# Hybrid decoder step: six weight buffers for the down products, half-size tiles for the sums, and loads of the next chunk's operands kept behind weight loads

## The chip, the core and the metric

The kernel runs on one core of one Trainium2 chip. The metric is the device time of one execution in microseconds (us). The kernel before took 3053.38 us, the median of three runs (3050.13 to 3064.35).

## The reference, cut to what matters

One layer of a hybrid decoder is computed for 512 prompt tokens and 8 sample tokens that share all weights (520 columns). The change lies in the last part, the feed-forward net:

```
FFN_HIDDEN = 5632
h2 = rms_norm(x, n2)
x = x + (jax.nn.silu(h2 @ wg) * (h2 @ wu)) @ wd
...
return (rms_norm(x, norm_f), ...)
```

`wg` and `wu` are 2048 x 5632 and `wd` is 5632 x 2048, all float32. The change touches only `... @ wd`, the down products.

## The kernel before, in words

**Precision.** Every product is made of three matmuls of split numbers: a weight block is split into a high part (`whi`, written by ACT at L1358) and the rest (`wlo`, written by DVE in `lo_part`, L70), the moving operand likewise, and hi*hi, hi*lo and lo*hi are added in PSUM (L1363).

**Seven products in place of eight.** The feed-forward products run through `strassen` (L1332), which multiplies a 2 x 2 arrangement of weight blocks `a11, a12, a21, a22` with seven operands named B11, B21, T2, T1, T3, T4 and B22. One call is called a step here. A step of the down products takes two weight tiles (`raws`, one for each of two output columns of blocks; the first holds a11 and a12, the second a21 and a22), and `kp` rows of block pairs. In order it makes:

- part A: a12 x B21 into PSUM tile `pz`, then a11 x B11 into `px`;
- part B: the sum s1 = a21 + a22 (POOL, L1342), s2 = s1 - a11 (DVE, L1352, into PSUM, named `sm`), then s2 x T2 into `px`, s1 x T1 into `py`; s4 = a12 - s2 (DVE, L1352, named `se`), s3 = a11 - a21 (POOL), s3 x T3 into `px`;
- part C: a22 x T4 into `px`, s4 x B22 into `py`.

After most products DVE adds PSUM to an accumulator in SBUF (`ac`, L1622). `run` (L1393) interleaves neighbours: part A of a step, part C of the step before, part B of the step. So on PE the order is A(j), C(j-1), B(j), A(j+1), C(j), ... The last reader of a step's second weight tile is the split of a22 in part C.

**The down products** (`streams`, L1682) go through the hidden dimension in six chunks of `CHUNKS = (3, 4, 4, 4, 3, 4)` block pairs (called chunks 1 to 6 here), and in each chunk through 8 steps, one for each pair of output blocks. A step of kp = 4 has 7 x 4 x 3 = 84 matmuls, one of kp = 3 has 63. The seven operands of a chunk come from DRAM (`load_x`, L1580, into halves of `wx` or into `hs` tiles, 1040 KB each at kp = 4); those of the next chunk are loaded while this chunk runs, one load behind each step in program order. The weights of a step (`load_w`, L1592) are two loads of 512 KB (kp = 4) or 384 KB (kp = 3) into `raw_c`, cut into four buffers taken in turn (L1598): two steps' worth. The tiles of the sums (`s`) come from pool `sp`, three buffers of 8 blocks, allocated for the up and gate products (kp = 8) and used on by the down products, which need half of it.

**What sets the order.** A scheduler places the instructions of each engine ahead of time, in an order fixed for the run; each engine then works through its list and waits at an instruction until its inputs are there and its buffer is free. All loads and stores are issued by one queue, SP's, in its own fixed order. `tc.keep_in_program_order` forbids the scheduler to move an instruction ahead of those that stand before it in the program on the same queue. When the first `hs` tile is needed (`hs`, L1545), the pools of the up and gate products are closed and their memory is given to `hs`.

Of the kernel before, what the change touches and what calls it, by code (L numbers as in the profile page):

```python
# [9 lines left out]
F32 = mybir.dt.float32  # L10
# [7 lines left out]
P = 128  # L18
# [4 lines left out]
HF = T // 2  # L23
# [10 lines left out]
def hybrid_step_kernel(  # L34
# [9 lines left out]
    nc = tc.nc  # L44
# [1094 lines left out]
    t = g_s5  # L1139
# [95 lines left out]
    XS = {}  # L1235
# [3 lines left out]
    def parts(x, q):  # L1239
        return x[:, q, 0:HF], x[:, q, HF:T]  # L1240
# [88 lines left out]

    todo = []  # L1330

    def strassen(A_, kp, X, parts_of, sp, rep):  # L1332

        groups = [(q0, min(4, kp - q0)) for q0 in range(0, kp, 4)]

        def comb(a, b, op):  # L1340
            t = sp.tile([P, (kp + 3) // 4 * 4, P], F32, tag="s", name="s")[:, 0:kp]
            G.tensor_tensor(t, a, b, op)  # L1342
            return [t[:, q0:q0 + n] for q0, n in groups]

        def pieces(a):
            return [a[:, q0:q0 + n] for q0, n in groups]

        def comb_ps(a, b, tag):

            t = [pmt("s" + tag, tag)[:, 0:n * P].rearrange("p (k m) -> p k m", m=P) for _, n in groups]  # L1350
            for t_, a_, b_ in zip(t, a, b):
                V.tensor_tensor(t_, a_, b_, ALU.subtract)  # L1352
            return t

        def prod(o, w, name, start=True):
            for (q0, n), w_in_ in zip(groups, w):
                hi, lo = parts_of(n)
                A.activation(hi, w_in_, AF.Copy)  # L1358
                lo_part(lo, w_in_, hi)
                for q in range(q0, q0 + n):  # L1360
                    xhi, xlo = X(name, q)
                    for i, (w_, x_) in enumerate(((hi, xhi), (hi, xlo), (lo, xhi))):
                        PE.matmul(o, w_[:, q - q0], x_, start=start and q == 0 and i == 0, stop=q == kp - 1 and i == 2,  # L1363
                                  skip_group_check=not start)
            if todo:
                todo.pop(0)()

        a11, a12, a22 = pieces(A_[0][0]), pieces(A_[0][1]), pieces(A_[1][1])
        z = bank("z")
        prod(z, a12, "B21", start=not rep("pre", z))  # L1370
        rep("p2", z)
        x = bank("x", 2)
        prod(x, a11, "B11")
        rep("11", x)
        yield
        s1 = comb(A_[1][0], A_[1][1], ALU.add)
        s2 = comb_ps(s1, a11, "m")
        prod(x, s2, "T2", start=False)
        rep("u2", x)
        y = bank("y")  # L1380
        prod(y, s1, "T1")
        s4 = comb_ps(a12, s2, "e")
        s3 = comb(A_[0][0], A_[1][0], ALU.subtract)
        prod(x, s3, "T3", start=False)
        rep("u3", x)
        rep("22", y)
        yield
        prod(x, a22, "T4", start=False)
        rep("21", x)
        prod(y, s4, "B22", start=False)  # L1390
        rep("12", y)
# [18 lines left out]
    NP = FF // (2 * P)  # L1410
# [2 lines left out]
    r2 = halves(rstd2)  # L1413
    wp_s.close()
    ww = ctx.enter_context(tc.tile_pool(name="ww", bufs=5, side="right"))
    sp = ctx.enter_context(tc.tile_pool(name="sp", bufs=3, side="right"))
    rms2 = sp.tile([P, T], F32, name="rms2", bufs=1)
    wq_s = ctx.enter_context(ExitStack())
    wq = wq_s.enter_context(tc.tile_pool(name="wq", bufs=4, side="right"))
# [76 lines left out]
    def up_or_gate(i, up):  # L1496
# [4 lines left out]
        def rep(step, o):  # L1501
# [23 lines left out]
            if step == "12":  # L1525
                if up:
                    split_hidden(i, c)
                else:
                    A.activation(c, c, AF.Silu)
                    sgate[0] = c  # L1530
        g = strassen(A_, 8, lambda name, q: parts(XS[name], q), wparts, sp, rep)
        yield next(g)
        if first[0]:
            rows(rstd2, rt)
# [2 lines left out]
        yield next(g)  # L1537
        next(g, None)

    run(up_or_gate(i, up) for i in range(NP) for up in range(2))  # L1540

    HW = 8 * HF
    hs_ = []

    def hs():  # L1545
        if not hs_:
            while todo:
                todo.pop(0)()
            fp_s.close()
            wq_s.close()  # L1550
            hs_.append(ctx.enter_context(tc.tile_pool(name="hs", bufs=6)))
        return hs_[0]

    with ExitStack():
        def flat(ap):
            return ap.rearrange("p a b -> p (a b)")
# [23 lines left out]
        def load_x(c):  # L1580

            X = {}
            for name in NAMES:
                X[name] = half()
                nc.sync.dma_start(X[name].bitcast(F32)[:, 0:CHUNKS[c]], xsc[c][name])
                yield X

        def load_acc(i):
# [3 lines left out]
        def load_w(q0, kp, i, first=False):  # L1592
            A_ = []
            for n in range(2):
                if first:
                    raw = wq.tile([P, 8, P], F32, tag="raw", name="raw", bufs=7)[:, 0:2 * kp]
                else:
                    r = nth("raw", 4)  # L1598
                    raw = raw_c[:, r * 1024:r * 1024 + 2 * kp * P].rearrange("p (k m) -> p k m", m=P)
                nc.sync.dma_start(raw, w_ffn_down[2 * q0 * P:2 * (q0 + kp) * P, (2 * i + n) * P:(2 * i + n + 1) * P]  # L1600
                                  .rearrange("(k p) m -> p k m", p=P))
                v = raw.rearrange("p (q h) m -> p h q m", h=2)
                A_.append([v[:, 0], v[:, 1]])
            return A_

        def down(c, q0, kp, i, X, A_=None):
# [14 lines left out]
                    j = (int(step[0]) - 1) * 2 + int(step[1]) - 1  # L1621
                V.tensor_tensor(a[:, j], o, a[:, j], ALU.add)  # L1622

            yield from strassen(A_, kp, lambda name, q: (X[name][:, q, 0], X[name][:, q, 1]), wparts, sp, rep)
            if c + 1 == len(CHUNKS):
                finish_pair(i, [flat(a[:, 2 * n:2 * n + 2]) for n in range(2)])

# [118 lines left out]
```

## Time and profile before

| what | value |
|---|---|
| median of three runs | 3053.38 us |
| profiled execution, its own time | 3053.86 us |
| span of that execution, first to last instruction | 3052.1 us |
| PE (matmul) busy | 2905.4 us, 95% |
| PEld (weight loads into PE) busy | 2860.4 us, 94% |
| DVE busy | 2035.9 us, 67% |
| ACT busy | 1275.5 us, 42% |
| POOL busy | 1142.2 us, 37% |
| mean granted TensorE clock | 0.976 of full speed |
| first and last matmul of the down products | 2520 and 3032 us |

The span is what the profile shows; 1.8 us of the execution lie outside it. A matmul's busy time overlaps that of the next one, so a stretch in which PE looks nearly busy can still have made fewer matmuls than it could: the number of matmuls in a stretch tells more than the busy share.

### The profile page before, as it was taken

What the parts mean: (1) busy time and instruction counts of PE and PEld (TensorE: products, weight loads), DVE (VectorE), ACT (ScalarE), POOL (GpSimd) and SP (SyncE); (2) the same over time, 40 slices, a digit from 0 to 9 for tenths busy, and PEclk for the clock granted to TensorE, in tenths of its full rate; (3) what the DMA queues carried; (4) which work ended last, traced back from release to release, by engine and by line L of the source; (5) the groups of instructions that cost most, each with busy time, mean ns of one, the idle gap of its engine ahead of it and who ended that gap; (6) DMA issues with size and microseconds to landing.
All of it is one profiled execution on the core that took longest, in us unless ns stands there. A gap on an engine that the chain in (4) does not pass through costs nothing.

```text
span 3052.1 us, 60983 instructions
## 1 busy us (share of the span) xinstructions
PE 2905.4 (95%) x23869; PEld 2860.4 (94%) x23869; DVE 2035.9 (67%) x3405; ACT 1275.5 (42%) x2229; POOL 1142.2 (37%) x1656
## 2 busy tenths in 40 slices
PE   8999999999999999799998999999999998999997
PEld 7999999999999999699998999999999998899997
DVE  6766434444554334343477999999999887788887
ACT  5344433233333232122254555555555554444455
POOL 0664303544445200210143555555555542222233
PEclk9999999899999998899998999999999999999999
DMA  6445443223333364744444555555555457555532
GB/s 161 106 124 133 123 122 98 68 73 76 80 81 87 90 195 110 177 142 121 122 126 135 157 164 164 162 166 163 161 164 174 150 191 271 184 198 164 183 97 97
DMA packets 647702, 424.17 MB, mean 139 GB/s; under 512 B 66526, under 2 KB 597695, under 8 KB 643775
## 3 DMA queue, kind: packets, MB, share of 16 engines
q1 hardware_dynamic: 647414, 420.28, 47.7%
q8 instruction: 188, 3.08, 0.4%
q14 instruction: 100, 0.81, 0.1%
HBM read 342.85 MB, written 75.12 MB: 137 GB/s over the span
## 4 chain that ended last, share of the span: by engine, by line
PE 70%; POOL 10%; DMA 8%; DVE 7%; issue 3%; ACT 1%; SPq 1%; POOLq 0%; ACTq 0%; DVEq 0%
PE pt L94 28%; PE px L1363 21%; PE py L1363 11%; PE pz L1363 6%; DVE wlo L70 3%; POOL tm L953 3%; POOL uu L955 2%; DMA dx<-xdsc 2%; DMA vb<-vsc 2%; DMA raws<-in_w_ffn_down_dram 2%; DVE sm L1352 1%; DVE ac L1622 1%; PE pss L904 1%; POOL et L597 1%; POOL et L598 1%
## 5 line engine op out<-in xcount | busy, mean ns | idle before, releaser
L70 DVE TENSOR_TENSOR wlo<-raw,whi 128x512 fp32r<-128x512 f32 (+1 forms) x485 | 524.1, 1095 | 244.4 <-ACT whi L78 196.8
L78 ACT ACTIVATE whi<-raw 128x1024 fp32r<-128x1024 f32 x218 | 231.0, 1060 | 672.1 <-PE pt L94 588.2
L94 PE MATMUL pt<-hhi,wlo 128*128 128x260 f32 (+2 forms) x2336 | 492.7, 289 | 4.4 <-DVE wlo L70 4.3
L94 PE MATMUL pt<-hlo,whi 128*128 128x260 f32 (+2 forms) x2336 | 493.8, 289 | 0.0
L94 PE MATMUL pt<-hhi,whi 128*128 128x260 f32 (+1 forms) x2336 | 489.9, 289 | 1.4 <-ACT pre L866 1.3
L94 PEld LDWEIGHTS pt<-hhi,wlo 128*128 128x128 f32 x2336 | 369.5, 191 | 7.9 <-DVE wlo L70 5.6
L94 PEld LDWEIGHTS pt<-hhi,whi 128*128 128x128 f32 x2336 | 367.7, 191 | 4.1 <-ACT pre L866 1.8
L94 PEld LDWEIGHTS pt<-hlo,whi 128*128 128x128 f32 x2336 | 370.1, 191 | 1.5 <-issue 0.2
L70 DVE TENSOR_TENSOR wlo<-s,whi 128x512 fp32r<-128x512 f32 (+1 forms) x272 | 318.7, 1186 | 1.4 <-ACT whi L1358 1.1
L1342 POOL TENSOR_TENSOR s<-raw 128x1024 f32<-128x1024 f32 (+1 forms) x90 | 217.2, 2415 | 250.3 <-DVE wlo L70 119.6
L1363 PE MATMUL px<-xT,whi 128*128 128x260 f32 x1408 | 258.0, 283 | 1.1 <-ACT u L1509 1.1
L1342 POOL TENSOR_TENSOR s<-raws 128x512 f32<-128x512 f32 (+1 forms) x94 | 122.5, 1317 | 333.2 <-DMA raws<-in_w_ffn_down_dram 194.9
L1358 ACT ACTIVATE whi<-s 128x512 fp32r<-128x512 f32 (+1 forms) x272 | 166.8, 618 | 171.3 <-PE px L1363 80.1
L1358 ACT ACTIVATE whi<-raw 128x512 fp32r<-128x512 f32 (+1 forms) x267 | 166.4, 630 | 125.4 <-PE px L1363 69.9
L1363 PEld LDWEIGHTS px<-xT,whi 128*128 128x128 f32 x1408 | 217.5, 189 | 1.3 <-ACT u L1509 1.3
L1363 PE MATMUL px<-xT,wlo 128*128 128x260 f32 x704 | 199.1, 283 | 0.0
L1363 PE MATMUL px<-wx,whi 128*128 128x260 f32 x832 | 160.5, 288 | 11.1 <-DVE ac L1622 5.3
L1363 PEld LDWEIGHTS px<-wx,whi 128*128 128x128 f32 x832 | 129.8, 191 | 15.5 <-ACT whi L1358 10.9
L1363 PE MATMUL pz<-xB,whi 128*128 128x260 f32 x704 | 131.1, 283 | 2.4 <-ACT whi L1358 2.4
L1363 PEld LDWEIGHTS px<-xT,wlo 128*128 128x128 f32 x704 | 132.6, 188 | 0.0
L1363 PE MATMUL py<-xT,whi 128*128 128x260 f32 x704 | 130.4, 285 | 0.1
L1358 ACT ACTIVATE whi<-sm 128x512 fp32r<-128x512 f32 (+1 forms) x136 | 79.7, 586 | 121.0 <-PE px L1363 70.0
(580 smaller groups left out, 7635.0 us busy)
## 6 DMA issues: line engine op xcount, KB each, us to landing
raw<-in_w_in_dram SPq DMA_DIRECT2D x146, 512.0 KB
raw<-in_w_ffn_gate_dram SPq DMA_DIRECT2D x88, 512.0 KB
raw<-in_w_ffn_up_dram SPq DMA_DIRECT2D x88, 512.0 KB
raws<-in_w_ffn_down_dram SPq DMA_DIRECT2D x64, 512.0 KB
xT<-hx SPq DMA_DIRECT2D x88, 260.0 KB
xB<-hx SPq DMA_DIRECT2D x66, 260.0 KB
raw<-in_w_out_dram SPq DMA_DIRECT2D x32, 512.0 KB
hs<-xT SPq DMA_DIRECT2D x12, 1040.0 KB
```

Of the source, the lines that this page charges most:

```text
L70: V.tensor_tensor(out, full, hi.bitcast(F32), ALU.subtract)
L78: A.activation(hi[:, :nk], raw[:, :nk], AF.Copy)
L94: PE.matmul(pt[:, h, 0:c1 - c0], w_[:, j], x[:, c0:c1], start=k == 0 and i == 0, stop=k == n - 1 and i == 2)
L597: G.tensor_tensor(t1[:, r, :, 0:n], E[:, r, :, 0:n], rr, ALU.mult)
L598: G.tensor_tensor(t2[:, r, :, 0:n], E[:, 1 - r, :, 0:n], ri, ALU.mult)
L904: PE.matmul(pss[:, s * 4 + c:s * 4 + c + 1], sq[:, s, c * P:(c + 1) * P], ones[:, 0:1], start=True, stop=True)
L953: G.tensor_tensor(tm[:, :, 0:31 - j], uu[:, :, j:j + 1].to_broadcast(sh), dx[:, j, j + 1:32].unsqueeze(1).to_broadcast(sh), ALU.mult)
L955: G.tensor_tensor(uu[:, :, j + 1:32], uu[:, :, j + 1:32], tm[:, :, 0:31 - j], ALU.add)
L1342: G.tensor_tensor(t, a, b, op)
L1352: V.tensor_tensor(t_, a_, b_, ALU.subtract)
L1358: A.activation(hi, w_in_, AF.Copy)
L1363: PE.matmul(o, w_[:, q - q0], x_, start=start and q == 0 and i == 0, stop=q == kp - 1 and i == 2, skip_group_check=not start)
```

## The change

- `load_w` takes six weight buffers in turn in place of four once the pools of the up and gate products are closed: the four in `raw_c` and two more (`rawx`) in a new pool `sd`.
- The sums' tiles come from pool `sd` from then on, three of 4 blocks in place of three of 8 blocks; pool `sp` is closed with the others. The two `rawx` tiles take memory that is free by this.
- Each load of an operand of chunks 2 to 6 (c > 0) is kept in program order, so behind the weight loads that stand before it in the program.
- `strassen` loses its argument `sp`. The rest moves lines only.

```
 def comb(a, b, op):
-    t = sp.tile([P, (kp + 3) // 4 * 4, P], F32, tag="s", name="s")[:, 0:kp]
+    t = s_tile(kp)
     G.tensor_tensor(t, a, b, op)
...
-    sp = ctx.enter_context(tc.tile_pool(name="sp", bufs=3, side="right"))
+    sp_s = ctx.enter_context(ExitStack())
+    sp = sp_s.enter_context(tc.tile_pool(name="sp", bufs=3, side="right"))
...
             fp_s.close()
             wq_s.close()
+            sp_s.close()
             hs_.append(ctx.enter_context(tc.tile_pool(name="hs", bufs=6)))
+            hs_.append(ctx.enter_context(tc.tile_pool(name="sd", bufs=3)))
         return hs_[0]
+    def s_tile(kp):
+        if hs_:
+            return hs_[1].tile([P, 4, P], F32, tag="sd", name="s")[:, 0:kp]
+        return sp.tile([P, 8, P], F32, tag="s", name="s")[:, 0:kp]
...
                 X[name] = half()
-                nc.sync.dma_start(X[name].bitcast(F32)[:, 0:CHUNKS[c]], xsc[c][name])
+                d = nc.sync.dma_start(X[name].bitcast(F32)[:, 0:CHUNKS[c]], xsc[c][name])
+                if c:
+                    tc.keep_in_program_order(d)
...
-                    r = nth("raw", 4)
-                    raw = raw_c[:, r * 1024:r * 1024 + 2 * kp * P].rearrange("p (k m) -> p k m", m=P)
+                    r = nth("raw", 6 if hs_ else 4)
+                    if r < 4:
+                        raw = raw_c[:, r * 1024:r * 1024 + 2 * kp * P].rearrange("p (k m) -> p k m", m=P)
+                    else:
+                        raw = hs_[1].tile([P, 8, P], F32, tag="rawx", name="rawx", bufs=2)[:, 0:2 * kp]
```

**Place 1: SP's queue where chunk 2 runs and the operands of chunk 3 are loaded.** `raws` and `rawx` are weight tiles (two loads a step), `wx0` to `wx3` the halves that hold chunk 3's operands (`xB212` is B21 of that chunk, `xT22` is T2, and so on). Before:

```order
L1600 DMA raws_30758<-in_w_ffn_down_dram 128x8x128 x2
L1585 DMA wx0_30754<-xB212_18393 128x2080
L1585 DMA wx0_30754<-xB112_18392 128x2080
L1600 DMA raws_30758<-in_w_ffn_down_dram 128x8x128
L1585 DMA wx1_30755<-xT22_18394 128x2080
L1600 DMA raws_30758<-in_w_ffn_down_dram 128x8x128
L1585 DMA wx2_30756<-xT32_18396 128x2080
L1585 DMA wx1_30755<-xT12_18395 128x2080
L1600 DMA raws_30758<-in_w_ffn_down_dram 128x8x128
L1585 DMA wx2_30756<-xT42_18397 128x2080
```

Now:

```order
L1613 DMA raws_30758<-in_w_ffn_down_dram 128x8x128 x2
L1613 DMA rawx_31840<-in_w_ffn_down_dram 128x8x128
L1613 DMA rawx_31842<-in_w_ffn_down_dram 128x8x128
L1593 DMA wx0_30754<-xB212_18393 128x2080
L1593 DMA wx0_30754<-xB112_18392 128x2080
L1613 DMA raws_30758<-in_w_ffn_down_dram 128x8x128 x2
L1593 DMA wx1_30755<-xT22_18394 128x2080
L1613 DMA raws_30758<-in_w_ffn_down_dram 128x8x128 x2
L1593 DMA wx1_30755<-xT12_18395 128x2080
L1613 DMA rawx_32244<-in_w_ffn_down_dram 128x8x128
```

Two weight loads, a whole step's, now stand between two operand loads from the second on; before it was one or none.

**Place 2: DVE's queue in a step of chunk 3.** `sm` is s2 of a step, `wlo<-raws` or `wlo<-rawx` the split of a weight block, `ac` the additions. The rows run from one s2 to the next split of a22, after which a step's second weight tile is free. Before, that split is the last row, `wlo_32408`:

```order
L1352 TENSOR_TENSOR sm_32443<-s_32441,raws_30758 128x512
L1622 TENSOR_TENSOR ac1_30759<-px_32255,ac1_30759 128x260
L70 TENSOR_TENSOR wlo_32350<-s_32347,whi_32349 128x512
L1622 TENSOR_TENSOR ac0_30757<-px_32121,ac0_30757 128x260
L70 TENSOR_TENSOR wlo_32373<-raws_30758,whi_32372 128x512
L1622 TENSOR_TENSOR ac0_30757<-py_32194,ac0_30757 128x260
L70 TENSOR_TENSOR wlo_32391<-raws_30758,whi_32390 128x512
L1622 TENSOR_TENSOR ac1_30759<-px_32255,ac1_30759 128x260
L70 TENSOR_TENSOR wlo_32408<-raws_30758,whi_32407 128x512
```

Now (with seven rows ahead of the s2) that split is the last row, `wlo_32420`; the s2, `sm_32589`, belongs to the step two after the one whose a22 is split:

```order
L70 TENSOR_TENSOR wlo_32342<-s_32319,whi_32341 128x512
L1635 TENSOR_TENSOR ac0_30757<-py_32204,ac0_30757 128x260
L1635 TENSOR_TENSOR ac1_30759<-px_32267,ac1_30759 128x260
L70 TENSOR_TENSOR wlo_32362<-s_32359,whi_32361 128x512
L1635 TENSOR_TENSOR ac0_30757<-px_32131,ac0_30757 128x260
L70 TENSOR_TENSOR wlo_32385<-raws_30758,whi_32384 128x512
L1635 TENSOR_TENSOR ac0_30757<-py_32204,ac0_30757 128x260
L1352 TENSOR_TENSOR sm_32589<-s_32587,raws_30758 128x512
L70 TENSOR_TENSOR wlo_32403<-raws_30758,whi_32402 128x512
L1635 TENSOR_TENSOR ac1_30759<-px_32267,ac1_30759 128x260
L70 TENSOR_TENSOR wlo_32420<-rawx_32246,whi_32419 128x512
```

The s2 is now made a whole step ahead of its own split. Within the step it stands behind the split of s3 and the additions that follow it, ahead of which it stood before, and two instructions in place of seven lie between it and the split of a22.

## Rows read from the trace of the kernel before

**Rows 1.** The page: busy time of each engine, share, instructions.

```profile
PE 2905.4 (95%) x23869; PEld 2860.4 (94%) x23869; DVE 2035.9 (67%) x3405; ACT 1275.5 (42%) x2229; POOL 1142.2 (37%) x1656
```

**Rows 2.** Windows: gate and up products, then chunks 1 to 6; us, busy (instructions) PE, PEld, DVE, ACT, POOL; clock, DMA share, GB/s.

```profile
1700.00:2400.00 700.00, 699.86 (x5831) 699.68 (x5830) 644.93 (x883) 383.17 (x730) 372.69 (x259) 1.00 0.54 163
2520.00:2593.00 73.00, 62.10 (x468) 59.69 (x467) 55.57 (x112) 32.18 (x73) 19.49 (x19) 0.95 0.77 264
2593.00:2684.00 91.00, 82.96 (x664) 81.39 (x663) 71.19 (x122) 39.51 (x72) 22.58 (x17) 0.98 0.58 190
2684.00:2771.00 87.00, 83.45 (x672) 81.05 (x671) 72.63 (x119) 39.67 (x72) 24.38 (x18) 1.00 0.55 180
2771.00:2861.00 90.00, 84.86 (x676) 81.80 (x675) 73.93 (x122) 39.47 (x72) 23.09 (x17) 1.00 0.50 157
2861.00:2931.00 70.00, 64.37 (x517) 62.29 (x516) 58.44 (x120) 33.46 (x72) 16.50 (x17) 1.00 0.55 181
2931.00:3033.00 102.00, 97.62 (x791) 94.19 (x790) 87.90 (x145) 62.96 (x129) 39.58 (x28) 1.00 0.24 69
```

**Rows 3.** One tile's instructions, chunk 2: the first product of its steps, first to last.

```profile
L1363 PE MATMUL pz<-hs,whi x64: 277/283/420, 2593.3 to 2675.2; 128*128 128x260 f32 x64
```

**Rows 4.** Waits of PE, down products: total us, times, longest.

```profile
PE pz L1363 <- DVE wlo L70: 12.6, 12, 3.8
PE px L1363 <- DVE ac L1622: 11.1, 15, 1.3
```

**Rows 5.** Chain that ended last, chunk 2: start us, us, what.

```profile
2633.84 3.62 DMA raws<-in_w_ffn_down_dram
...
2637.60 1.31 POOL s L1342
...
2638.93 1.77 DVE sm L1352
...
2643.20 3.80 DMA raws<-in_w_ffn_down_dram
...
2651.14 0.34 DVE ac L1622
2651.48 0.60 DVE wlo L70
```

**Rows 6.** The same chain in chunk 5 (kp = 3).

```profile
2907.77 3.24 DMA raws<-in_w_ffn_down_dram
...
2911.15 1.30 POOL s L1342
...
2912.48 1.36 DVE sm L1352
...
2914.63 0.47 DVE wlo L70
...
2916.73 3.31 DMA raws<-in_w_ffn_down_dram
```

**Rows 7.** Waits of POOL and of DVE, 2520 to 3033 us.

```profile
POOL s L1342 <- DMA raws<-in_w_ffn_down_dram: 194.9, 27, 14.2
```
```profile
DVE sm L1352 <- POOL s L1342: 18.7, 16, 3.2
```

**Rows 8.** Timeline of SP's queue in chunk 1: start us, us, issues.

```profile
2548.13 0.90 SPq L1585 DMA_DIRECT2D hs<-xT  x2
2549.13 0.68 SPq L1600 DMA_DIRECT2D raws<-in_w_ffn_down_dram  x1
```

**Rows 9.** Timeline of POOL in chunk 1, idle time before in brackets.

```profile
2560.51 1.95 POOL L1342 TENSOR_TENSOR s<-raws 128x384 f32<-128x384 f32 x2 [14.24 <-DMA raws<-in_w_ffn_down_dram]
```

**Rows 10.** Groups of DVE instructions, 2620 to 2960 us: count, busy us, mean ns, idle before.

```profile
L70 DVE TENSOR_TENSOR wlo<-s,whi 128x512 fp32r<-128x512 f32 x49 | 50.5, 1040 | 0.2 <-ACT whi L1358 0.2
L70 DVE TENSOR_TENSOR wlo<-raws,whi 128x512 fp32r<-128x512 f32 x72 | 49.5, 689 | 0.9
```

**Rows 11.** Waits of SP's queue, 2600 to 2700 us.

```profile
SPq L1585 <- PE pz L1363: 7.1, 1, 7.1
```

More of the change, by code (lines that the diff above doesn't have):

```diff
@@ L1330, in hybrid_step_kernel, with strassen @@
     todo = []
-    def strassen(A_, kp, X, parts_of, sp, rep):
+    def strassen(A_, kp, X, parts_of, rep):
         groups = [(q0, min(4, kp - q0)) for q0 in range(0, kp, 4)]
         def comb(a, b, op):
-            t = sp.tile([P, (kp + 3) // 4 * 4, P], F32, tag="s", name="s")[:, 0:kp]
+            t = s_tile(kp)
             G.tensor_tensor(t, a, b, op)
@@ L1530, in rep @@
                     sgate[0] = c
-        g = strassen(A_, 8, lambda name, q: parts(XS[name], q), wparts, sp, rep)
+        g = strassen(A_, 8, lambda name, q: parts(XS[name], q), wparts, rep)
         yield next(g)
@@ L1538, in up_or_gate @@
         next(g, None)
-    run(up_or_gate(i, up) for i in range(NP) for up in range(2))
-    HW = 8 * HF
     hs_ = []
@@ L1550, in hs @@
             wq_s.close()
+            sp_s.close()
             hs_.append(ctx.enter_context(tc.tile_pool(name="hs", bufs=6)))
+            hs_.append(ctx.enter_context(tc.tile_pool(name="sd", bufs=3)))
         return hs_[0]
+    def s_tile(kp):
+        if hs_:
+            return hs_[1].tile([P, 4, P], F32, tag="sd", name="s")[:, 0:kp]
+        return sp.tile([P, 8, P], F32, tag="s", name="s")[:, 0:kp]
+    run(up_or_gate(i, up) for i in range(NP) for up in range(2))
+    HW = 8 * HF
     with ExitStack():
@@ L1622, in rep @@
                 V.tensor_tensor(a[:, j], o, a[:, j], ALU.add)
-            yield from strassen(A_, kp, lambda name, q: (X[name][:, q, 0], X[name][:, q, 1]), wparts, sp, rep)
+            yield from strassen(A_, kp, lambda name, q: (X[name][:, q, 0], X[name][:, q, 1]), wparts, rep)
             if c + 1 == len(CHUNKS):
```

## The prediction

> **What bounds the kernel now.** I read the page first, then windows, then waits and the chain of waits, and at last the queues' timelines. By the page PE is the bound: 95% busy [rows 1]. The change touches only the down products, so the windows come next. During the gate and up products PE makes 5831 matmuls in 700 us, one every 0.120 us, and never rests, with DVE at 92% [rows 2]. In the down products it falls short. The windows are cut where the first product of a chunk begins, as 2593.3 for chunk 2 [rows 3]. At 0.120 us for a matmul, the matmuls of each window account for so much of it [rows 2]:
>
> - chunk 1: 468 x 0.120 = 56.2 of 73 us, 16.8 lost (clock 0.95 there, some 3.7 of the loss)
> - chunk 2: 79.7 of 91, 11.3 lost
> - chunk 3: 80.7 of 87, 6.3 lost
> - chunk 4: 81.2 of 90, 8.8 lost
> - chunk 5: 62.1 of 70, 7.9 lost
> - chunk 6: 95.0 of 102, 7.0 lost (the end's transposes are among its matmuls, so this is rough)
>
> Together 58 us: nothing that helps only here can gain more. PE's own waits name DVE, its splits (12.6 us) and its additions (11.1 us) [rows 4], yet DVE is at 78 to 86% in these windows, less than the 92% at which PE never rests. DVE is late at moments, not overloaded. The chain says what it is late for: weight load 3.62, sum on POOL 1.31, s2 on DVE 1.77, some splits and additions of 0.60 and 0.34, and the next load begins the moment the split of a22 ends, 9.36 us after the one before [rows 5]. In chunk 5 the same ring takes 8.96 us from load to load [rows 6]. PE alone would need 84 x 0.120 = 10.1 us for a step of chunk 2 and 63 x 0.120 = 7.6 us for one of chunk 5. So in chunk 5 the ring is the bound. In chunk 2 its length depends on how many instructions DVE has between s2 and the split: with the seven of place 2 it is 1.77 + 4 x 0.34 + 3 x 0.60 + 0.60 + 3.80 + 1.31 = 10.6 us, above PE's 10.1. POOL waits 194.9 us for weights in all, and DVE stands 18.7 us at an s2 for POOL's sum, with the additions queued behind it that PE waits for [rows 7].
>
> **The change part by part.**
>
> *Six buffers and the new order on DVE.* The ring gets a step more of slack. Now two instructions lie between s2 and the split of a22, and the s2 is one for two steps on: 1.77 + 0.60 + 0.34 + 0.60 + 3.80 + 1.31 = 8.4 us a step [rows 5], 1.7 less than PE's 10.1. For kp = 3: 1.36 + 0.47 + 0.34 + 0.47 + 3.31 + 1.30 = 7.25 us [rows 5, 6], only 0.3 less than PE's 7.6; one addition more in between and they are equal. So the ring stops being the bound, narrowly at kp = 3. The s2 also no longer stands ahead of the additions that PE needs soonest, and what it can still wait for is a sum made a step before.
>
> What is late next is the play between DVE, ACT and PE: a split waits for PE to give back one of five split buffers, an addition waits for PE, PE waits for the addition. The trace doesn't show a down step free of the ring, so I bound what remains. From below: nothing, as in the gate and up products, where the same code makes PE rest not at all [rows 2]. From above: chunk 3, the least disturbed, lost 6.3 us in 8 steps, 0.8 a step. A step here has products half as long as there, so DVE has half the time for an addition; I take the middle, 0.4 a step, 3.2 a chunk. For chunk 5, where ring and PE are nearly equal, I take 0.5, so 4.0. That gives 11.3 - 3.2 = 8.1 in chunk 2, 3.1 in chunk 3, 5.6 in chunk 4, 3.9 in chunk 5. Chunk 6 has no operand loads, and its transposes, squares and copies stay; I give it 2 of its 7.
>
> *The pinned loads.* They remove no bytes. In chunk 1 a weight load was issued behind three operand loads of 1040 KB [rows 8], and POOL stood 14.24 us for it [rows 9]. A step of 7.6 us leaves POOL 7.6 - 1.95 = 5.6 us idle anyway, so 14.24 - 5.6 = 8.6 us were lost. By the order now, seven weight loads stand between the fourth one of the stage and the first `hs` load, so this wait should go: 8.6. But six `hs` loads then stand together ahead of the weights of later steps, so I leave chunk 1 its other 8.2. In chunks 2 to 5 the operand loads now go out one for each step. Their hiding place is the rest of their chunk; a load issued in the seventh step still has more than a step, over 7.6 us, before its product. The price of a store or load moved past another is therefore nothing, unless it blocks SP (a rival below).
>
> *The sums' tiles.* As many buffers as before and the same sums of the same size: nothing. The closing of the old pools falls where the `hs` tiles closed the others already; nothing. Outside the down products the order is the same row for row, line numbers aside; nothing there.
>
> **Sum**: 8.6 + 8.1 + 3.1 + 5.6 + 3.9 + 2.0 = 31.3 us. Against the profiled execution, 3053.9 - 31.3 = 3022.6; the median of the runs is 0.5 lower, so I say 3023.
>
> *One rule against it.* A split of a sum, which DVE makes mostly while POOL is busy, takes 1040 ns; a split of a weight block takes 689 [rows 10]. So POOL beside it costs DVE 0.35 us. The Trainium skill (GPSIMD Engine Reference, Specifications) says that GpSimd shares its SBUF interfaces with VectorE and contends with DVE instructions that have two SBUF inputs. The trace agrees as far as these two rows go. POOL's sums are as many as before, so the row's 0.35 is paid as often in my sum; by the rule alone it only moves. Where it moves is the third rival.
>
> **The rivals.**
>
> 1. *No rest remains* (as in the gate and up products): chunks 2 to 5 give back all of 11.3 + 6.3 + 8.8 + 7.9 = 34.3, with 8.6 and 2.0 that is 44.9: 3009 us. For it: DVE's share. Against: half-length products and kp = 3.
> 2. *The play of DVE and PE is the bound, not the ring*: every step of chunks 2 to 5 goes on losing chunk 3's 0.8, so 6.4 a chunk (chunk 3 none gained): 4.9 + 0 + 2.4 + 1.5 = 8.8, and half of chunk 1's 8.6: 13 us, 3041. For it: PE's waits name additions too [rows 4]. The change not doing what it says (the new tiles late, because the old pools still hold their memory) would look the same, but the loads into them stand from the third step on.
> 3. *POOL's sums meet the wrong splits.* Freed from the weights' arrival, POOL's two sums run beside whatever DVE does. If both slow a split for which PE waits, 2 x 0.35 = 0.7 us a step [rows 10], over the 40 steps of chunks 2 to 6, take back 28 us: 3051. By the Trainium skill's rule above that is possible on any split. Against: a split is usually made several products ahead of its matmuls.
> 4. *Slower: SP blocked by its pinned loads.* An operand load that waits for PE to free its half now holds all weight loads behind it, and the scheduler can't lift these over it. Such a wait was 7.1 us at its longest [rows 11]. It decides once it is longer than the lead that the extra buffers give. If at the start of each of chunks 2 to 5, where the halves fall free, weights come late by it: 4 x 7.1 = 28.4 us on top of the old time, 3082. Against: in the order, the product that frees a half comes before the split that frees the weight buffer behind it.
>
> **How the numbers follow.** Forecast 0.50 (own range 3012 to 3034), rival 1 0.18, rival 2 0.15, rival 3 0.12, rival 4 0.05. A measurement of this kernel can tell about 0.5%, 15 us, from no change: below 3038 is faster. That is the forecast, rival 1 and nearly half of rival 2: 0.75. Same has the rest of rival 2 and most of rival 3: 0.18. Slower has rival 4 and a little of rival 3: 0.07. The range leaves out rival 4 and the outer parts of rivals 1 and 3: 3007 to 3048.
>
> **What would show it.** Right: DVE's wait at s2 for POOL falls from 18.7 us to a few; weight loads leave the chain in chunks 2 to 5; chunks 2 to 4 take about 83 us each and chunk 5 about 66; PE makes over 95% of its 0.120 us rate there; POOL's 14.24 in chunk 1 is gone; operand loads are spread over a chunk. Wrong: PE's waits for `ac` and `wlo` as long as before with weights on time (rival 2), weight-block splits of 1 us (rival 3), SP waiting long at operand loads while POOL waits for weights (rival 4). The prediction fails if the weights arrive on time and the steps of chunks 2 to 4 still take 11 us.

## The result, and the profile after

| | before | after |
|---|---|---|
| median of the runs taken side by side | 3051.76 us (4 runs, 3043.82 to 3064.35) | 3009.77 us (4 runs, 3003.06 to 3018.45) |
| ratio after to before, 95% interval | | 0.9861, 0.9837 to 0.9885 |
| profiled execution, its span | 3053.86, 3052.1 us | 3003.06, 3001.3 us |

The change makes the kernel faster by 42 us, 1.4%. The prediction said 3023 (3007 to 3048): the sign and the range hold, the gain was taken too small.

The profiled spans differ by 50.8 us. Of that 6.6 us lie before the down products (their first product starts at 2513.4 us, before at 2520.0), where the instructions stand in the same order; single runs of either kernel scatter by 15 to 20 us, and no cause is looked for there. The other 44.2 us lie in the down products. The page's busy times, which answer to [rows 1], hardly move:

```profile
PE 2884.6 (96%) x23869; PEld 2848.7 (95%) x23869; DVE 2043.5 (68%) x3405; ACT 1279.8 (43%) x2229; POOL 1132.9 (38%) x1656
```

The windows by chunk, with the columns of [rows 2] (cut at the first product of each chunk; chunk 6 up to 2983):

```profile
2513.00:2582.00 69.00, 60.73 (x472) 57.39 (x471) 58.81 (x115) 32.29 (x73) 24.77 (x22) 1.00 0.88 305
2582.00:2661.00 79.00, 79.00 (x661) 79.00 (x660) 73.65 (x121) 39.92 (x72) 21.45 (x16) 1.00 0.65 209
2661.00:2742.00 81.00, 81.00 (x678) 81.00 (x677) 74.33 (x123) 40.38 (x73) 20.71 (x16) 1.00 0.59 199
2742.00:2822.00 80.00, 80.00 (x669) 80.00 (x669) 72.81 (x121) 39.92 (x72) 19.83 (x16) 1.00 0.52 170
2822.00:2887.00 65.00, 64.28 (x524) 62.88 (x522) 62.17 (x119) 35.03 (x73) 17.06 (x16) 1.00 0.60 198
2887.00:2983.00 96.00, 94.97 (x787) 93.50 (x787) 85.97 (x146) 64.28 (x130) 35.59 (x27) 1.00 0.22 62
```

In chunks 2 to 4 PE is busy for the whole of each window and makes a matmul every 0.120 us (678 in 81 us), as in the gate and up products. DVE is at 91 to 93% there, where before it was at 78 to 84% [rows 2]. In chunk 5 DVE is at 96%. The chain of waits of chunk 3 names PE alone, where the pieces shown of before went from weight load to weight load [rows 5, 6]:

```profile
2664.31 4.32 PE px L1363 x36
...
2674.40 4.29 PE px L1363 x36
```

From 2664.31 to 2674.40 is one step: 10.1 us. In chunk 5 the chain from 2855.8 on is DVE's own work, splits, additions and s2 without a load or a sum between them, in a step of 7.77 us (from s2 to s2) against PE's 7.6:

```profile
2856.34 0.42 DVE sm L1352
...
2864.11 0.42 DVE sm L1352
```

Waits over the down products (2515 to 2990 us), PE's first, which answer to [rows 4], then POOL's [rows 7]:

```profile
PE pz L1363 <- DVE wlo L70: 4.8, 6, 1.7
PE px L1363 <- DVE ac L1635: 1.3, 4, 0.6
```
```profile
POOL s L1342 <- DVE wlo L70: 275.3, 82, 7.2
POOL s L1342 <- DMA rawx<-in_w_ffn_down_dram: 20.7, 2, 13.3
```

DVE's wait at s2 for POOL, 18.7 us before, is gone from DVE's list (the longest there are now 25.6 us for `whi` and 6.9 us for `px`), and POOL now waits mostly for DVE to give back a sum's tile, for weights only 28 us (20.7 of them in the row above). SP's waits at the operand loads, which answer to [rows 11], are all short:

```profile
SPq L1593 <- PE py L1363: 4.9, 15, 0.5
SPq L1593 <- PE px L1363: 2.8, 5, 1.0
```

### The profile page after: what moved, and what is told of

It reads as the page before. It is cut to its first block, busy times and chain, and to the rows that moved or that the text cites. A ratio compares the mean times of both kernels' runs of the same rounds, so it can differ in the third digit from the quotient of the medians.

```text
span 3001.3 us, 60983 instructions
## 1 busy us (share of the span) xinstructions
PE 2884.6 (96%) x23869; PEld 2848.7 (95%) x23869; DVE 2043.5 (68%) x3405; ACT 1279.8 (43%) x2229; POOL 1132.9 (38%) x1656
## 4 chain that ended last, share of the span: by engine, by line
PE 76%; POOL 8%; DMA 6%; DVE 5%; issue 2%; ACT 1%; SPq 1%; POOLq 0%; ACTq 0%; DVEq 0%
PE pt L94 30%; PE px L1363 23%; PE py L1363 12%; PE pz L1363 6%; POOL tm L953 2%; DVE wlo L70 2%; POOL uu L955 2%; DMA vb<-vsc 2%; DMA dx<-xdsc 2%; PE pss L904 1%; POOL et L598 1%; DVE ac L1635 1%; POOL et L597 1%; PE psk L761 1%; DVE sm L1352 0%
## 5 line engine op out<-in xcount | busy, mean ns | idle before, releaser
L1342 POOL TENSOR_TENSOR s<-raw 128x1024 f32<-128x1024 f32 (+1 forms) x90 | 217.3, 2415 | 254.9 <-DVE wlo L70 121.1
L1358 ACT ACTIVATE whi<-raw 128x512 fp32r<-128x512 f32 (+1 forms) x267 | 166.2, 630 | 125.7 <-PE px L1363 68.8
L1342 POOL TENSOR_TENSOR s<-raws 128x512 f32<-128x512 f32 (+1 forms) x64 | 80.3, 1257 | 193.0 <-DVE wlo L70 192.1
L1363 PE MATMUL px<-xB,whi 128*128 128x260 f32 x704 | 129.5, 283 | 0.2 <-ACT whi L1358 0.2
```

## The experiments

Each run is judged by its median and by its chunks. The table gives the length of each chunk, from its first product (into `pz`) to that of the next chunk, and for chunk 6 to the end of the span, all from the profiled execution of each kernel. Ratios are to the kernel before on the same chip. Chunk 1's start is blurred, since its first product may lie among the last up products; there chunks 1 and 2 are best read together.

| kernel | 1 | 2 | 3 | 4 | 5 | 6 | median us | ratio, 95% interval |
|---|---|---|---|---|---|---|---|---|
| before | 73.3 | 90.8 | 87.4 | 89.9 | 70.2 | 120.5 | 3051.8 | |
| the change | 68.8 | 79.1 | 80.6 | 80.6 | 64.1 | 114.7 | 3009.8 | 0.9861 (0.9837 to 0.9885) |
| six buffers, no pins | 69.6 | 79.7 | 80.9 | 80.6 | 65.1 | 114.8 | 3009.4 | 0.9857 (0.9840 to 0.9874) |
| pins alone | 72.4 | 89.7 | 87.0 | 87.7 | 70.8 | 119.7 | 3054.6 | 0.9998 (0.9981 to 1.0014) |
| half-size tiles alone | 73.2 | 87.1 | 85.8 | 90.0 | 70.2 | 121.1 | 3048.0 | 0.9989 (0.9979 to 0.9999) |
| five buffers | 70.6 | 81.7 | 81.2 | 80.6 | 66.7 | 113.0 | 3014.7 | 0.9886 (0.9871 to 0.9901) |
| two tiles for sums | 65.8 | 83.7 | 83.4 | 83.5 | 63.7 | 115.4 | 3017.5 | 0.9893 (0.9872 to 0.9914) |
| each load twice | 92.2 | 86.2 | 88.4 | 92.5 | 78.8 | 116.1 | 3075.8 | 1.0077 (1.0060 to 1.0093) |
| before, short loads | 73.3 | 90.7 | 86.8 | 83.9 | 68.6 | 115.4 | 3037.7 | 0.9952 (0.9938 to 0.9967) |
| the same, with pins | 71.4 | 86.8 | 83.4 | 83.9 | 67.6 | 116.4 | 3034.7 | 0.9919 (0.9901 to 0.9936) |
| all loads pinned | 72.4 | 81.7 | 80.6 | 80.9 | 67.3 | 114.8 | 3019.7 | 0.9897 (0.9880 to 0.9914) |
| all but two steps' weights | 71.7 | 81.0 | 80.6 | 80.9 | 65.9 | 114.8 | 3020.7 | 0.9869 (0.9850 to 0.9888) |
| accumulators pinned | 64.9 | 82.8 | 80.6 | 80.6 | 64.1 | 115.0 | 3007.9 | 0.9826 (0.9810 to 0.9842) |

**The parts apart.** Six buffers without the pins, against the change:

```
-                d = nc.sync.dma_start(X[name].bitcast(F32)[:, 0:CHUNKS[c]], xsc[c][name])
-                if c:
-                    tc.keep_in_program_order(d)
+                nc.sync.dma_start(X[name].bitcast(F32)[:, 0:CHUNKS[c]], xsc[c][name])
```

> The change without its pins: six weight buffers and half-size tiles, the operand loads free to move as before. Ring theory (load, sum on POOL, s2, splits, split of a22 bound a step; more buffers break it, the pins matter in chunk 1 at most): chunks 2 to 5 last 79 to 81, 80 to 81, 80 to 81 and 64 to 65 us as with the whole change, chunk 1 68 to 73 us, in all 3008 to 3018 us. Burst theory (operand loads sent together hold up the weights, and the pins cure that): chunks 2 to 4 stay at 86 to 91 us, chunk 5 at 68 to 70, in all 3038 to 3050 us. Order theory (DVE's new order alone does it): as the ring theory, since DVE's order is nearly the new one here.

The pins alone, against the kernel before:

```
-                nc.sync.dma_start(X[name].bitcast(F32)[:, 0:CHUNKS[c]], xsc[c][name])
+                d = nc.sync.dma_start(X[name].bitcast(F32)[:, 0:CHUNKS[c]], xsc[c][name])
+                if c:
+                    tc.keep_in_program_order(d)
```

> The kernel before with the pins alone: four weight buffers, full-size tiles. Ring theory: chunks 2 to 4 stay at 85 to 90 us each and chunk 5 at 68 to 70, with weight loads still in the chain of waits; chunk 1 may gain a few us; in all 3038 to 3052 us. Burst theory: chunks 2 to 4 fall to 80 to 82 us and chunk 5 to 64 to 65, in all 3010 to 3020 us. Order theory: as the ring theory, since DVE's order is nearly the old one.

The half-size tiles alone: the change without the pins, and with

```
-                    r = nth("raw", 6 if hs_ else 4)
+                    r = nth("raw", 4)
```

> The kernel before with the half-size tiles of the sums and the earlier closing of their old pool alone; DVE's and POOL's order in the stage reads as before. All theories: nothing, chunks 2 to 6 within 1 us each of those before (91, 87, 90, 70 and 122 us), in all 3045 to 3058 us. If the tiles' place in memory mattered, chunks 2 to 5 would be shorter by several us each.

Measured: the two added buffers are the change. Without the pins the time is the same (0.9857 beside 0.9861). The pins alone bring nothing (0.9998), the tiles alone about nothing (0.9989; chunks 2 and 3 are some 4 and 1.5 us shorter there, more than expected, in chunk 2 all of it at its border to chunk 1). The burst theory falls.

The run with pins alone shows more than that. Its expectation was weight loads still in the chain of waits. The chain's shares by line over its chunks 3 and 4 (2680 to 2853 us) hold no load and no sum:

```profile
by line: PE px L1363 44.2%; PE py L1363 25.3%; PE pz L1363 14.1%; DVE wlo L70 7.5%; DVE ac L1624 2.3%; DVE se L1352 2.0%; DVE sm L1352 1.8%; ACT whi L1358 1.5%; issue 1.3%; DVEq L70 0.1%; ACTq L1358 0.0%
```

And yet its steps took 8.6, 12.0 and 12.5 us in turn, 10.9 on average. A piece of that chain at a late step:

```profile
2805.11 0.69 DVE se L1352
2805.80 0.33 DVE ac L1624
2806.13 1.62 DVE wlo L70
2807.75 0.61 DVE sm L1352
2808.36 0.34 DVE ac L1624
...
2808.84 1.68 PE px L1363 x12
```

DVE's waits of the same kernel in chunks 3 and 4:

```profile
DVE ac L1624 <- PE px L1363: 13.2, 11, 1.9
DVE wlo L70 <- ACT whi L1358: 10.0, 21, 0.7
DVE wlo L70 <- PE py L1363: 8.1, 5, 1.6
```

No instruction of DVE waits for a sum or a weight. PE waits for the addition at 2808.36, ahead of which DVE first makes a split that takes 1.62 us (POOL makes a sum at the same moment) and the s2. So here the order of DVE's work, with a sum of POOL's beside a split, costs the time, not the arrival of the weights. That is the prediction's second rival with a part of its third, in a kernel with four buffers.

**Sooner or later weights.** The kernel before with short loads: from the third step of chunk 2 on a weight load leaves out all but two of its eight (six) blocks, so the down products are computed with partly old weights.

```
+                k = 2 if q0 and (q0 > 3 or i > 1) else 2 * kp
-                nc.sync.dma_start(raw, w_ffn_down[2 * q0 * P:2 * (q0 + kp) * P, (2 * i + n) * P:(2 * i + n + 1) * P]
+                nc.sync.dma_start(raw[:, 0:k], w_ffn_down[2 * q0 * P:(2 * q0 + k) * P, (2 * i + n) * P:(2 * i + n + 1) * P]
```

> The kernel before with its four buffers and old tiles, but from the third step of chunk 2 on each weight load brings only the first two of its eight (six) blocks, 128 KB in place of 512 or 384; the other blocks of a tile are what was left there, so the down products are computed with partly old weights. No instruction less on any engine; only the weights come sooner (some 2 us in place of 3.8). DVE's order stays of the old kind, s2 ahead of a row of additions, though not row for row that of before. Ring theory: 10.6 - 1.8 = 8.8 us a step, under PE's 10.1, so chunks 3 and 4 last 80 to 83 us, chunk 5 64 to 66, in all 3010 to 3025 us. Order theory (DVE's old order alone costs the time, and six buffers help by letting the scheduler change it): chunks 3 and 4 stay at 86 to 90, in all 3035 to 3050 us.

Measured 3037.7. The time lies in the range of the order theory, and so does chunk 3 (86.8); chunk 4 (83.9) lies between the two theories. Most steps of chunks 3 and 4 took 10.1 to 10.9 us, the longest 14.6. So I added the pins to it, as in the diff above:

> The kernel with short weight loads (four buffers, old tiles, 128 KB in place of 512 or 384 from the third step of chunk 2 on, so computed with partly old weights) with the operand loads kept in program order as well: between two operand loads stand two weight loads. In the run with short loads alone most steps of chunks 3 and 4 took 10.1 to 10.9 us, one a chunk 14.6, where a weight load lay beside operand loads and took 4.8 us in place of 2.3. If four buffers are short of slack for such a burst (ring theory): the step of 14.6 goes, chunks 3 and 4 last 81 to 83 us, in all 3015 to 3030 us. If the long step comes from DVE's order: it stays, chunks 3 and 4 last 84 to 87 us, in all 3033 to 3042 us.

Measured 3034.7, again in the range of the order theory (3033 to 3042), though the step of 14.6 went, as the ring theory had it. Chunk 3 fell to 83.4 and chunk 4 stayed at 83.9, between the two theories. Between steps of 10.1 stand some of 10.5 to 11.4. What is late in those shows in the chain of waits, in chunk 4 of the run with short loads and pins:

```profile
2795.21 0.70 DVE wlo L70
...
2795.93 2.62 DMA raws<-in_w_ffn_down_dram
...
2798.69 1.30 POOL s L1342
...
2800.02 0.70 DVE sm L1352
2800.72 0.34 DVE ac L1625
```

It is the ring again with a load of 2.62 us: split of a22, load, sum, s2, and behind the s2 the addition that PE waits for. A ring without lead cost time here even where its sum was under 10.1 us, because s2 came just in time and held up what stood behind it.

The other way round, the change with each load issued twice (the second waits for the first):

```
+                for _ in range(1 if first else 2):
-                nc.sync.dma_start(raw, w_ffn_down[2 * q0 * P:2 * (q0 + kp) * P, (2 * i + n) * P:(2 * i + n + 1) * P]
+                    nc.sync.dma_start(raw, w_ffn_down[2 * q0 * P:2 * (q0 + kp) * P, (2 * i + n) * P:(2 * i + n + 1) * P]
```

> The whole change, with every weight load of the down products (but the first step's) issued twice into the same tile, the second after the first has landed: it doubles the time from a free tile to its weights and adds bytes, no arithmetic. Ring theory: a step's ring grows from 8.4 to 8.4 + 3.8 = 12.2 us at kp = 4 and from 7.25 to 7.25 + 3.3 = 10.6 us at kp = 3, over PE's 10.1 and 7.6, so chunks 2 to 4 last some 97 us each, chunk 5 some 84, chunk 6 some 17 us more than now, in all about 3090 to 3110 us. If instead the weights now land a step or more ahead with nothing tied to them (no ring left), it hides: chunks within 2 us of now, in all 3005 to 3020 us.

Measured 3075.8. Chunks 3 and 4 took 88.4 and 92.5 us, 11.3 a step, neither 10.1 (hidden) nor 12.2 (fully on the path). DVE stood at s2 for POOL's sum again in those chunks, 2.4 us each time:

```profile
DVE sm L1352 <- POOL s L1342: 38.1, 16, 4.4
```

So the six buffers hide part of a doubled load and not all. DVE's order was another one in this kernel too, and the doubled bytes raised the DMA share of these chunks from 0.56 to 0.82, so the 11.3 can't be split between order, lateness and bytes. Chunk 1 lost most (92.2 us), at a DMA share of 0.93 (0.88 with the change).

**How much lead.** Five buffers, against the change:

```
-                    r = nth("raw", 6 if hs_ else 4)
+                    r = nth("raw", 5 if hs_ else 4)
-                        raw = hs_[1].tile([P, 8, P], F32, tag="rawx", name="rawx", bufs=2)[:, 0:2 * kp]
+                        raw = hs_[1].tile([P, 8, P], F32, tag="rawx", name="rawx", bufs=1)[:, 0:2 * kp]
```

> The whole change with five weight buffers in place of six. The second tile of a step is then loaded when the first tile of two steps before is free, about half a step sooner than with four; some loads still wait for the split of a22. Ring theory: most of the gain is there, chunks 2 to 4 last 80 to 84 us, in all 3010 to 3025 us. If the ring is only open with a full step of lead, chunks 2 to 4 last 85 to 90 us, in all 3030 to 3050 us.

Two tiles for the sums, against the change:

```
-            hs_.append(ctx.enter_context(tc.tile_pool(name="sd", bufs=3)))
+            hs_.append(ctx.enter_context(tc.tile_pool(name="sd", bufs=2)))
```

> The whole change with two tiles for the sums in place of three, so that a sum can't be made a step ahead; in DVE's order the split of a22 and the s2 then stand further apart again. Six buffers as in the change. Ring theory: weights still have a step of lead, so nothing is lost: chunks 2 to 4 last 79 to 82 us, in all 3005 to 3020 us. Order theory (the gain is the s2 made a step ahead): chunks 2 to 4 go back to 85 to 90 us, in all 3030 to 3045 us.

Measured: five buffers have nearly all of it (3014.7; steps of 10.07 in most of chunks 2 to 4, the rest lost in chunks 1, 2 and 5). With two tiles for the sums every step of chunks 3 and 4 takes 10.40 to 10.45 us in place of 10.07, and PE makes its 1345 matmuls of those chunks in 166.8 us where the change takes 161.1:

```profile
2668.40:2835.20 166.80, 165.53 (x1345) 162.20 (x1345) 147.69 (x243) 80.27 (x144) 40.84 (x32) 1.00 0.55 181
```

The time (3017.5) lies in the range of the ring theory, the chunks (83.4 to 83.7) between the two: the loss is 0.35 a step, not 1 and not 0. Where it lies is seen in the groups of DVE's instructions, chunks 3 and 4. First the kernel before, then the change, then two tiles for the sums:

```profile
L70 DVE TENSOR_TENSOR wlo<-s,whi 128x512 fp32r<-128x512 f32 x32 | 37.3, 1170 | 0.0
L70 DVE TENSOR_TENSOR wlo<-raws,whi 128x512 fp32r<-128x512 f32 x47 | 31.9, 679 | 0.8
L1352 DVE TENSOR_TENSOR sm<-s,raws 128x512 f32<-128x512 f32 x16 | 17.1, 1067 | 4.5 <-POOL s L1342 4.5
```
```profile
L70 DVE TENSOR_TENSOR wlo<-raws,whi 128x512 fp32r<-128x512 f32 x32 | 32.2, 1005 | 0.0
L70 DVE TENSOR_TENSOR wlo<-s,whi 128x512 fp32r<-128x512 f32 x32 | 32.1, 1002 | 2.1 <-ACT whi L1358 0.2
L1352 DVE TENSOR_TENSOR sm<-s,raws 128x512 f32<-128x512 f32 x10 | 6.8, 684 | 0.0
```
```profile
L70 DVE TENSOR_TENSOR wlo<-raws,whi 128x512 fp32r<-128x512 f32 x32 | 21.6, 675 | 0.0
L1352 DVE TENSOR_TENSOR sm<-s,raws 128x512 f32<-128x512 f32 x11 | 18.3, 1667 | 0.0
```

With two tiles every s2 runs beside a sum of POOL's and takes 1667 ns. With three, s2 takes 684 and the splits of weight blocks 1005 in place of 679. In the run with two tiles the slow s2 stands in the chain of waits, step after step, right ahead of the split that PE waits for:

```profile
2708.28 1.59 DVE sm L1352
2709.87 0.60 DVE wlo L70
...
2710.51 1.47 PE pz L1363 x10
```

In the change the same contention falls on splits made ahead of need, and PE never rests.

**Chunk 1.** It still loses some 8 us (68.8 against 63 x 8 x 0.120 = 60.5), most of it in its third step (12.05 us), its fifth (9.5) and its last two (9.6 and 10.6). All loads kept in program order, against the change:

```
-                nc.sync.dma_start(flat(accs[i][:, 2 * n:2 * n + 2]), asc[2 * i + n])
+                tc.keep_in_program_order(nc.sync.dma_start(flat(accs[i][:, 2 * n:2 * n + 2]), asc[2 * i + n]))
...
-                nc.sync.dma_start(raw, w_ffn_down[2 * q0 * P:2 * (q0 + kp) * P, (2 * i + n) * P:(2 * i + n + 1) * P]
+                d = nc.sync.dma_start(raw, w_ffn_down[2 * q0 * P:2 * (q0 + kp) * P, (2 * i + n) * P:(2 * i + n + 1) * P]
...
+                if not first:
+                    tc.keep_in_program_order(d)
```

> The whole change with the loads of the accumulators and of all weights of the down products kept in program order as well, so that in chunk 1 two weight loads, two accumulator loads and one operand load take turns on SP's queue in place of six operand loads in a row. Nothing else. If the order of the loads costs chunk 1 its remaining 8 us: chunk 1 lasts 62 to 66 us in place of 68.8, the other chunks as now, in all 3003 to 3007 us. If chunk 1 is held by the bytes it moves (a DMA share near 1.0 at its start): chunk 1 stays at 67 to 71 us, in all 3008 to 3013 us. If the pins hold weights back behind a blocked load: chunk 1 over 72 us.

Measured 3019.7, 10 us worse than the change (the intervals of the ratios just touch, at 0.9880 and 0.9885): the third expectation, with chunk 1 just over its 72 us. Chunk 1's last six steps took 7.5 to 8.8 us, as hoped, but its second took 17.6. In the timeline of SP's queue four stores of chunk operands (L1458) stand ahead of the next pinned loads and wait for DVE, which makes the halves that they store (11.5 us of waits for `hx` there); the third step's weights go out 15 us after the first of them:

```profile
2525.78 9.63 SPq L1458 DMA_DIRECT2D xT<-hx  x4
...
2540.49 1.01 SPq L1613 DMA_DIRECT2D raws<-in_w_ffn_down_dram  x2
```

So I let the weights of the second and third step move up again:

```
-                if not first:
+                if q0 or i > 2:
                     tc.keep_in_program_order(d)
```

> The kernel in which all loads are kept in program order, but with the weight loads of the second and third step of chunk 1 free to move up again. There the second step took 17.6 us, since its weights were issued behind the stores and loads of chunk 1's own operands, and the last steps of chunk 1 took 7.5 each. Expected: the second step as with the change (6 to 9 us), the last five 7.5 to 8 each, chunk 1 61 to 65 us, in all 3002 to 3008 us. If the weights of the fourth step are now the late ones: one step of 12 to 17 us remains, chunk 1 over 67 us, in all over 3010 us.

Measured 3020.7, the second outcome (by its ratio, 0.9869, it is not shown to be slower than the change): the same four stores (12.15 us on SP's queue) now held up the weights of the fourth step, whose first product comes 15.0 us after the third's. Last, the accumulators' loads alone in program order, the first line pair of the diff above:

> The whole change with the loads of the accumulators kept in program order, two to a step, in place of fifteen of sixteen ahead of the second step's end; the weight loads stay free to move up. If the bytes of the accumulators hold up chunk 1's third step (12.05 us there, the DMA share near 1.0): that step falls to 8 to 9 us, chunk 1 lasts 63 to 66 us, in all 3003 to 3008 us. If something else does (the last loads of chunk 1's own operands, the six operand loads in a row): chunk 1 stays at 67 to 71 us, in all 3008 to 3013 us.

Measured 3007.9, with chunk 1 at 64.9 and its third step at 6.5 us: the time and chunk 1 lie in the first expectation's ranges. But the second step grew to 14.9 us and chunk 2 to 82.8. From the first product of chunk 1 to that of chunk 6 it is 372.9 us here and 373.2 with the change, and the intervals of the ratios touch (0.9842 and 0.9837): no difference is shown, so this is not called a better version. Its windows around the start of chunk 1 show why little is to be had there:

```profile
2520.00:2530.00 10.00, 8.92 (x75) 8.71 (x74) 5.63 (x12) 4.66 (x11) 1.46 (x2) 1.00 1.01 354
2530.00:2540.00 10.00, 6.99 (x53) 6.49 (x53) 8.95 (x14) 5.50 (x14) 6.30 (x7) 0.93 1.04 365
2540.00:2550.00 10.00, 10.00 (x64) 10.00 (x64) 7.67 (x17) 4.17 (x10) 2.99 (x3) 0.73 0.93 287
```

The DMA share is 0.93 to 1.04 through these 30 us. With the accumulators sent later, the late load in the chain is a weight load (5.09 us) in place of an accumulator's (6.11 us). What is left in chunk 1 fits a limit by bytes; a run with fewer bytes there was not tried.

## Why the prediction was right or wrong

Its steps, against the chunks' lengths (gain by them, 44 us in all, forecast 31.3):

| chunk | forecast | measured |
|---|---|---|
| 1 | 8.6 | 4.5 |
| 2 | 8.1 | 11.7 |
| 3 | 3.1 | 6.8 |
| 4 | 5.6 | 9.2 |
| 5 | 3.9 | 6.1 |
| 6 | 2.0 | 5.8 |

*That six buffers are the part that pays:* right, shown by the run without pins and by the run with pins alone.

*The rest that I left:* this is the term that was mis-sized. "A step here has products half as long as there, so DVE has half the time for an addition; I take the middle, 0.4 a step, 3.2 a chunk." The steps of chunks 2 to 4 take 10.07 us, and 84 x 0.120 is 10.08: no rest. (Chunk 2 is shorter than 8 such steps, since its first one, 8.6 us, shares a border with chunk 1.) So in these chunks the first rival came true (3009, given 0.18), and the median lies just below the forecast's own range. That its 3009 is met so closely is luck in part: chunk 1 gained 4.1 us less than it said and chunk 6 3.8 more. In chunk 5 a rest of 3.6 us remains (64.1 against 60.5), nearly the 4.0 that I left it, but for another reason: not the ring beside PE, but DVE, which is at 96% there and makes up the chain from the middle of the chunk on. The lower bound had a row behind it, the gate and up products with DVE at 92% [rows 2]; that DVE is now at 91 to 93% in chunks 2 to 4 says the same. The upper bound, chunk 3's 0.8, came from a chunk in which the old order was still at work, so it was no measure of what remains without it. Halfway between a clean row and a disturbed one was no estimate.

*The ring as the cause:* half right. The chain of the kernel before did go through weight loads [rows 5, 6], and the row that I named, DVE's wait at s2, vanished. But with pins alone the same loss stands with no late weight in it, and in the kernel before itself weight loads are 3.3% of the chain over chunks 3 and 4, some 6 of 177 us:

```profile
by line: PE px L1363 37.3%; PE py L1363 21.3%; PE pz L1363 13.1%; DVE wlo L70 11.7%; DVE ac L1622 4.5%; DVE sm L1352 3.8%; DMA raws<-in_w_ffn_down_dram 3.3%; issue 2.3%; DVE se L1352 1.5%; POOL s L1342 0.7%; ACT whi L1358 0.7%; DVEq L70 0.0
```

I had read the two places where the chain did run through loads, and not its shares. What the ring sets is not only when weights come but which order is possible. Now DVE makes the s2 of a step ahead of the split of a22 two steps before it (place 2). With four buffers this order can't be: the weights for that s2 go into the very tile that the split still has to read. (With five they go into a tile that is free half a step sooner, and five brought nearly all.) So four buffers force s2 to come just in time, beside the additions that PE waits for, even when loads are quick. Two runs show a part of the gain each, in chunks 3 and 4, where the change gained 16.0 us (177.2 to 161.2). With short loads and pins in the old kernel 9.9 came (167.3) and 6.1 stayed. With six buffers but sums that can't be made a step ahead, 10.3 came (166.9) and 5.7 stayed. One could read from both that six tenths of the gain are for weights that come early and four tenths for a sum and an s2 that lie a step ahead, but other rows speak against it. With short loads and pins the weights still come just in time, and loads and sums are a larger part of the chain over chunks 3 and 4 than before:

```profile
by line: PE px L1363 34.3%; PE py L1363 19.0%; DMA raws<-in_w_ffn_down_dram 10.9%; DVE wlo L70 9.2%; PE pz L1363 7.8%; POOL s L1342 7.1%; DVE ac L1625 4.0%; DVE sm L1352 3.8%; ACT whi L1358 2.3%; issue 1.9%; POOLq L1342 0.1%
```

With the pins alone no load is in the chain, and 13.6 of the 16.0 us stay lost (174.8). And each of these kernels got a DVE order of its own from the scheduler. So it is shown that the two buffers bring the gain; how it divides between early weights and the order that they allow stays open.

*The ring's numbers:* the sums (10.6 for four buffers, 8.4 for six) were too stiff a picture. With doubled loads 8.4 + 3.8 = 12.2 was expected and 11.3 measured; with short loads 8.8 was expected, below PE's 10.1, and 10.7 (without pins) and 10.5 (with them) measured. A ring that crosses engines with other work in between neither bounds a step sharply nor disappears once its sum is below the bound.

*Chunk 1:* half as much as forecast. "... so this wait should go: 8.6." It did not go, it moved, from 14.24 us [rows 9] to 13.30 at one `rawx` tile:

```profile
2565.75 1.99 POOL L1342 TENSOR_TENSOR s<-rawx 128x384 f32<-128x384 f32 x2 [13.30 <-DMA rawx<-in_w_ffn_down_dram]
```

The six `hs` loads now stand together ahead of it, as the prediction noted, four of them in this row of SP's timeline and one on either side:

```profile
2545.02 1.84 SPq L1593 DMA_DIRECT2D hs<-xT  x4
```

The two steps from there on took 9.6 and 10.6 us in place of 7.6, so 5 us are still lost there; before, the one step with the wait took 15.2. Moving the burst did not remove its price here, with the DMA share near 1.0 (1.01 from 2550 to 2560, 0.97 in the 10 us behind). (DVE was at 76% in chunk 1 before [rows 2], not at 78 to 86% as in the other chunks.)

*Chunk 6:* 2 of 7 forecast, 5.8 measured. I kept most of it for the transposes, but a step with its transposes now takes 11.2 us, and PE makes its instructions without a rest (97 in 11.2 us):

```profile
2929.10:2940.30 11.20, 11.20 (x97) 11.15 (x96) 10.78 (x17) 7.62 (x16) 5.54 (x4) 1.00 0.30 85
```

The transposes are PE's work and were part of no loss. Before, the second to seventh steps took 11.2 to 12.8 us, now 10.6 to 11.6. The first seven steps give 4.4 of the 5.8 us, and 1.4 lie behind the first product of the last step.

*The third rival:* its mechanism happened and cost nothing. Weight-block splits did go to 1 us, as it said (0.69 to 1.005, above). A split is made ahead of its matmuls, as was argued against it; PE's waits for `wlo` fell from 12.6 to 4.8 us. "Any split" was too wide: a split of s4 begun beside a sum took 0.69 in the kernel before, one of s2 0.68 with the pins alone, the same as without a sum.

*The fourth:* the pinned operand loads wait 0.5 and 1.0 us at most at SP. It did not happen there. It did in the kernels with more pins, at another place: behind stores that wait for DVE.

*The signs named ahead:* DVE's wait at s2 gone (right), loads out of the chain of chunks 2 to 5 (right), chunks 2 to 4 at about 83 us (79 to 81), chunk 5 at about 66 (64.1), POOL's 14.24 in chunk 1 gone (wrong, 13.30), operand loads spread, one to a step (right, and of no worth: without the pins they go out in twos and the time is the same).

## What to carry to other kernels

A wait in a ring of buffers can cost more than the time an engine is seen to wait: a buffer too few also forbids the order in which the next step's small sums are made early, so an in-order engine meets them just in time, ahead of work that another engine needs. To size what a buffer brings, look for a stretch of the same code that runs undisturbed and take its rate as the end, not the mean with a disturbed one; then look which engine is next (here the rate was reached with DVE at 91 to 93%, and not in chunk 5 with DVE at 96%). And pin loads on a shared queue only after looking at what else stands in it: one store that waits for a busy engine holds up all loads pinned behind it.

## What the hardware showed that I had not expected

- A sum on POOL (1.3 us) holds up those of DVE's instructions that read both inputs from SBUF: splits of weight blocks and of sums, and s2. In chunks 3 and 4 of the change 31 such splits of 128x512 begin while a sum runs. Each of them ends 0.55 us after the sum does, and most take 1.33 or 1.65 us in place of 0.68. The 16 additions that begin beside a sum, with one input in PSUM, take 0.42 us, as they do alone. A row of POOL, then two of DVE (the sum ends at 2708.97, the split at 2709.52):

```profile
2707.67 1.30 POOL L1342 TENSOR_TENSOR s<-rawx 128x512 f32<-128x512 f32 x1 [6.85 <-DVE wlo L70]
```
```profile
2707.85 0.42 DVE L1635 TENSOR_TENSOR ac<-px,ac 128x260 f32<-128x260 f32 x1
2708.19 1.33 DVE L70 TENSOR_TENSOR wlo<-s,whi 128x512 fp32r<-128x512 f32 x1
```

  Over chunks 3 and 4, with 32 sums, the excess over 0.69 us an instruction is 32 x 0.48 + 16 x 0.38 = 21 us before (splits of sums, s2) and 32 x 0.31 + 32 x 0.32 + 16 x 0.29 = 25 us after (splits of sums and of both weight tiles; `rawx` at 983 ns): 0.67 and 0.78 us a sum. The excess is moved and not removed, and its place decides: with two tiles for the sums it falls on s2, which stands in the chain, and a step is 0.35 us longer; on early splits it cost nothing. (Whether all of the 0.35 is its doing, no run tells apart.) The Trainium skill (GPSIMD Engine Reference, Specifications) says that GpSimd shares its SBUF interfaces with VectorE and contends with DVE instructions that have two SBUF inputs; these rows agree and give the size here.
- A stretch in which PE rested was followed in some runs by a lower granted clock. In the run with the accumulators pinned (rows above) PE made 53 matmuls from 2530 to 2540 (clock 0.93), where 85 or 86 are the full rate in such a window; the next 10 us had a clock of 0.73, so part of them at the lower level of 1.2 GHz, and PE, busy throughout, made 64. There the wait is paid for a second time. It is not so each time: with the change PE made 55 in its slow 10 us and kept the full 2.4 GHz:

```profile
2530.00:2540.00 10.00, 7.55 (x55) 6.66 (x55) 7.61 (x18) 3.88 (x9) 2.75 (x3) 1.00 0.99 317
2540.00:2550.00 10.00, 9.11 (x72) 8.59 (x71) 9.77 (x19) 5.36 (x13) 3.04 (x3) 1.00 0.64 216
```
